# Four block sums of the up-projection weights: one by an adding DMA, two in place, and a new order of the seven products

## The chip, the cores and the metric

The kernel runs on one core of one Trainium2 chip. A core has TensorE (PE in the rows) for matrix products, VectorE (DVE), ScalarE (ACT) and GpSimd (POOL) for elementwise work, and 16 DMA engines that move data between HBM and the on-chip SBUF. SyncE (SP) only issues DMAs here. Each engine works through its own list of instructions in order and waits at semaphores for the others. The metric is the device time of one execution in microseconds (us).

## The reference

The kernel computes an encoder of two layers on a sequence of 512 rows of width 1024. Each layer is a half-step feed-forward block, a token mixer (a convolution module in layer 0, a gated linear recurrence "HGRN2" in layer 1), and a second half-step feed-forward block:

```
def swiglu(h, w13, w2):
    gate, up = jnp.split(h @ w13, 2, axis=-1)
    return (jax.nn.silu(gate) * up) @ w2

for layer in range(DEPTH):                       # DEPTH = 2
    x = x + 0.5 * swiglu(rms_norm(x, ...), ffn_w13[layer, 0], ffn_w2[layer, 0])
    x = x + mix(rms_norm(x, ...))                # conv in layer 0, HGRN2 in layer 1
    x = x + 0.5 * swiglu(rms_norm(x, ...), ffn_w13[layer, 1], ffn_w2[layer, 1])
return rms_norm(x, final_g)
```

There are thus four feed-forward blocks. `w13` has 2 x 2816 columns, in 22 blocks of 128 for the gate and 22 for the up half. The change touches the product `h @ w13` of all four blocks, and the storage of HGRN2's `v`.

## The kernel before

**Products in three parts.** All is fp32. A weight tile is split in `split` (L128-130) into a rounded part `whi` (a ScalarE copy, L129) and the rest `wlo` (a VectorE subtraction, L130); the activations are held as `x7h` and `x7l` in the same way. Each product is three matmuls: high by high, high by low, low by high.

**Seven products for eight.** The up-projections (`h @ w13`) use the Strassen-Winograd scheme: one gate block and one up block, each of 128 columns, form a *pair*, and a pair is one 2 x 2 block product, made with seven block products for eight. There are 86 pairs in all (22 in each of three feed-forward blocks, 20 in the first, where two pairs are done plainly). A pair's raw weights are one 128 x 2048 tile `wraw` of 1 MB with four quarters of 512 columns, a11, a12, a21, a22. SP loads it (L123-124, three buffers). `seven_w` (L154-173) makes four sums on VectorE, each 128 x 512:

- S1 = a21 + a22 and S2 = S1 - a11, in a tile `s12`;
- S4 = a12 - S2 and S3 = a11 - a21, in a tile `s43`.

It splits four weight tiles from these: wa = (S1, S2), wb = (a11, a12), wc = (S4, S3), each 128 x 1024, and wd = a22, 128 x 512 (`wdh`, `wdl`). wa, wb and wc take the `whi`/`wlo` buffers in turn, of which there are three (L152); wd has a buffer of its own.

**Order of the products.** `seven` (L449-456, matmuls at L455) issues one block product: 12 matmuls of 128 x 256. `seven_pair` (L458-509) issues those of a pair, 84 matmuls with wd's, into two PSUM tiles `x` and `y`: wa's first half, wb's first half, then wd of the *previous* pair (in `close`), wa's second half, wb's second half, wc's first and wc's second half. ScalarE copies parts between (L468-469, L492, L497), VectorE adds two 128 x 256 parts (L495, L498, recorded at L149), and the gate is formed in `evac`: t (L523, VectorE), silu (L525, ScalarE), t (L527, VectorE), gh (L528, ScalarE), gl (L529, VectorE). The first pair of a half block has no previous one (`close is None`) and runs its products in another order.

**What sets the order around the change.** The program's order is not the engines' order: the tile framework schedules each engine's list when the program is built, so instructions of pair n+1's weights stand between those of pair n's products. Buffers are taken in turn, and a writer waits until the last reader of the old content is through. In the steady stretches a pair's list repeats with only the buffer numbers changed.

**The other half** of a feed-forward block, `@ w2`, uses plain products with 512 columns (L187-189). Between the blocks come norms, whose sums of squares `ss` are added on POOL (L334).

Of the kernel before, what the change touches and what calls it, by code (L numbers as in the profile page):

```python
# [11 lines left out]
F32 = mybir.dt.float32  # L12
# [3 lines left out]
AF = mybir.ActivationFunctionType  # L16
ALU = mybir.AluOpType

P = 128
D = 1024  # L20
S = 512
# [39 lines left out]
def tile_encoder(ctx: ExitStack, tc: tile.TileContext, xT, vecs, masks, w13, w2, pw1, kout, kout2, win, win_i, out):  # L61
    nc = tc.nc
    cst = ctx.enter_context(tc.tile_pool(name="cst", bufs=1))
    xp = ctx.enter_context(tc.tile_pool(name="xp", bufs=1))
    wp = ctx.enter_context(tc.tile_pool(name="wp", bufs=3))
# [33 lines left out]
    for w_ in win_order:  # L99
        n = int(w_[1:])  # L100
# [4 lines left out]
    plan_kout(1)  # L105
    plan_ffn(3)

    raws = {}
    parts = []
    for ci, (src, sizes) in enumerate(plan):  # L110
        off = 0
# [4 lines left out]
    ready = {}  # L116

    def wdma(upto):
        while state["dma"] < min(upto, len(plan)):
            ci = state["dma"]  # L120
            src, sizes = plan[ci]
            n = sum(sizes)
            t = wp.tile([P, 2048], F32, name="wraw", tag="wraw", bufs=3)  # L123
            nc.sync.dma_start(t[:, :n], src)
            raws[ci] = t
            state["dma"] += 1

    def split(hi, lo, raw, off, a, b):  # L128
        nc.scalar.copy(hi[:, a:b], raw[:, off + a:off + b])  # L129
        nc.vector.tensor_tensor(lo[:, a:b], raw[:, off + a:off + b], hi[:, a:b].bitcast(F32), op=ALU.subtract)  # L130

    def wsplit(upto):
        while state["split"] < min(upto, len(parts)):
            i = state["split"]
            ci, off, sz = parts[i]
            wdma(ci + 1)
            if sz > D:
                ready[i] = seven_w(raws[ci])
                state["split"] += 1
                continue  # L140
            hi = wp.tile([P, D], F32R, name="whi", tag="whi", bufs=3)
            lo = wp.tile([P, D], F32R, name="wlo", tag="wlo", bufs=3)
            raw = raws[ci]
            split(hi, lo, raw, off, 0, sz)
            ready[i] = (hi, lo)
            state["split"] += 1

    def add(o, a, b, op=ALU.add):
        nc.vector.tensor_tensor(o, a, b, op=op)  # L149

    def wtile():
        return [wp.tile([P, D], F32R, name=n, tag=n, bufs=3) for n in ("whi", "wlo")]  # L152

    def seven_w(raw):  # L154


        q = D // 2
        a11, a12, a21, a22 = (raw[:, i * q:(i + 1) * q] for i in range(4))
        s12 = st["R"].tile([P, D], F32, name="s12", tag="s12")
        s43 = st["R"].tile([P, D], F32, name="s43", tag="s43")  # L160
        add(s12[:, :q], a21, a22)
        add(s12[:, q:], s12[:, :q], a11, ALU.subtract)
        wa = wtile()
        split(*wa, s12, 0, 0, D)
        wb = wtile()
        split(*wb, raw, 0, 0, D)
        add(s43[:, :q], a12, s12[:, q:], ALU.subtract)
        add(s43[:, q:], a11, a21, ALU.subtract)
        wc = wtile()
        split(*wc, s43, 0, 0, D)  # L170
        wd = [st["R"].tile([P, q], F32R, name=n, tag=n) for n in ("wdh", "wdl")]
        split(*wd, raw, 3 * q, 0, q)
        return wa, wb, wc, wd
# [21 lines left out]
    st = {}  # L195
# [28 lines left out]
    for k in range(0, KD, 2):  # L224
        sl = slice(k // 2 * P, (k // 2 + 1) * P)
        src = plan[0][0].rearrange("p (g c) -> p g c", g=4)[:, :, sl]
# [55 lines left out]
    norm = {}  # L282
# [166 lines left out]
    def seven(o, w, i, slot, start=False, kps=range(NP)):  # L449

        x = slice(slot * T2, (slot + 1) * T2)
        for kp in kps:
            sl = slice((i * NP + kp) * P, (i * NP + kp + 1) * P)
            for a, b in ((w[0], x7h), (w[0], x7l), (w[1], x7h)):
                nc.tensor.matmul(o, lhsT=a[:, sl], rhs=b[kp][:, x], start=start and kp == 0 and a is w[0] and b is x7h,  # L455
                                 stop=kp == NP - 1 and a is w[1], skip_group_check=True)

    def seven_pair(lead, close, done):  # L458


        wa, wb, wc, wd = wget()
        x, y = psum(), psum()
        l, r = slice(0, T2), slice(T2, S)
        cs = st["R"].tile([P, 3 * T2], F32, name="cs", tag="cs")
        p5, u2, u3 = (cs[:, i * T2:(i + 1) * T2] for i in range(3))

        def seed():
            nc.scalar.copy(y[:, l], x[:, l])  # L468
            nc.scalar.copy(p5, x[:, r])

        if close is None:
            z = psum()
            for kps in (range(NP - 1), range(NP - 1, NP)):
                seven(x[:, r], wa, 0, 1, True, kps)
                seven(x[:, l], wb, 0, 0, False, kps)
                if kps[-1] == NP - 1:
                    seed()
                seven(z[:, l], wb, 1, 2, True, kps)
                seven(z[:, r], wc, 0, 3, False, kps)
            lead.group()  # L480
            zs = tp.tile([P, S], F32, name="t0", tag="t0")
            nc.scalar.copy(zs, z)
            add(x, x, zs)
            seven(y[:, l], wa, 1, 5)
            nc.scalar.copy(u2, y[:, l])
        else:
            seven(x[:, r], wa, 0, 1, True)
            seven(x[:, l], wb, 0, 0)
            seed()
            close()  # L490
            seven(y[:, l], wa, 1, 5)
            nc.scalar.copy(u2, y[:, l])  # L492
            seven(x[:, l], wb, 1, 2)
            seven(x[:, r], wc, 0, 3)
        add(x[:, r], x[:, r], u2)  # L495
        seven(y[:, l], wc, 1, 4)
        nc.scalar.copy(u3, y[:, l])  # L497
        add(y[:, r], u3, p5)  # L498
        if close is None:
            lead.group()  # L500
        wnext()

        def end():
            seven(y[:, l], wd, 0, 6)
            if lead.n == 2:
                lead.group()
            done(x, y)()

        return end
# [314 lines left out]
    def hgrn(next_prep):  # L824
        lead = Lead()
        with tc.tile_pool(name="hn", bufs=1) as hn, ExitStack() as scratch:
            onh = [hn.tile([P, S], F32R, name=f"onh{k}", tag=f"onh{k}") for k in range(NH)]
            onl = [hn.tile([P, S], F32R, name=f"onl{k}", tag=f"onl{k}") for k in range(NH)]
            hp = scratch.enter_context(tc.tile_pool(name="hp", bufs=1))
# [24 lines left out]

            def v_proj(g, hook=None):

                v = hp.tile([P, 4, S], F32, name="v", tag="v")
                acc = [psum() for _ in range(4)]
                for part in range(4):
                    hi, lo = wget()  # L860
                    for c in range(4):
                        for kk in range(2):
                            k = part * 2 + kk
                            ts_ = slice(c * P, (c + 1) * P)
                            sl = slice(kk * S, (kk + 1) * S)
                            nc.tensor.matmul(acc[c], lhsT=xh[k][:, ts_], rhs=hi[:, sl], start=k == 0, stop=False)  # L866
                            nc.tensor.matmul(acc[c], lhsT=xh[k][:, ts_], rhs=lo[:, sl], start=False, stop=False)  # L867
                            nc.tensor.matmul(acc[c], lhsT=xl[k][:, ts_], rhs=hi[:, sl], start=False, stop=k == KD - 1)  # L868
                            if hook is not None:
                                hook()  # L870
                    lead.group()
                    wnext()
                for c in range(4):
                    nc.scalar.activation(v[:, c, :], acc[c], AF.Copy, scale=norm["r4"][:, c:c + 1])
                vt[g] = v

            def q_evac(h, p):
# [48 lines left out]
            def head(h):  # L926
                q, f, k, kd, gg = (T.pop((h, n)) for n in ("q", "f", "k", "kd", "gg"))

                A = hp.tile([P, 4, S // 2], F32, name="A", tag="A")
# [29 lines left out]
                while hl <= 128:  # L959
# [5 lines left out]
                    else:  # L965
                        for i, (s_, d_, t_) in enumerate(((0, 0, 1), (1, 1, 0), (2, 0, 3), (3, 1, 2))):
                            nc.tensor.matmul(sp[:, i * P:(i + 1) * P], lhsT=k[:, d_, s_ * P:(s_ + 1) * P],
                                             rhs=Q[:, 1 - d_, t_ * P:(t_ + 1) * P], start=True, stop=True)
# [47 lines left out]
                kts = hp.tile([P, S], F32, name="kts", tag="kp", bufs=2)  # L1016
                nc.scalar.copy(kts, kt)
                yield WIDE_STEP
                v = vt[h // 4]
                hs = slice((h % 4) * P, (h % 4 + 1) * P)  # L1020
                st = psum("aux")
                for s_ in range(4):
                    d_ = s_ // 2
                    nc.tensor.matmul(st[:, d_ * P:(d_ + 1) * P], lhsT=kts[:, s_ * P:(s_ + 1) * P], rhs=v[:, s_, hs],
                                     start=s_ % 2 == 0, stop=s_ % 2 == 1)
                state = hp.tile([P, 2 * P], F32, name="state", tag="state")
                nc.scalar.copy(state, st[:, :2 * P])
# [3 lines left out]
                for t_ in range(4):  # L1031
                    ot = po[:, t_ * P:(t_ + 1) * P]
                    a_ = t_ // 2
                    for c in (2 * a_, 2 * a_ + 1):
                        nc.tensor.matmul(ot, lhsT=A[:, c, (t_ % 2) * P:(t_ % 2 + 1) * P], rhs=v[:, c, hs],  # L1035
                                         start=c % 2 == 0, stop=False)
                    nc.tensor.matmul(ot, lhsT=Q[:, a_, t_ * P:(t_ + 1) * P], rhs=state[:, (1 - a_) * P:(2 - a_) * P],
                                     start=False, stop=True)
                    if t_ == 1:
                        yield 1  # L1040
# [205 lines left out]
```

## Time and profile before

| what | value |
|---|---|
| median of three runs | 2042.1 us (2040.7 to 2044.1) |
| the profiled execution: its own time, its span | 2041.71 us, 2039.9 us |
| TensorE busy | 1977.2 us, 97% of the span |
| VectorE busy | 1554.6 us, 76% |
| ScalarE busy | 1046.2 us, 51% |
| GpSimd busy | 253.7 us, 12% |
| read from HBM | 178.92 MB |

The span runs from the first to the last recorded instruction; the execution's own time has some 1.8 us more around it. A busy share is an average over stages of different kinds: the 86 pairs, the `w2` products, the two mixers and the norms. The line numbers in rows are those of the kernel before, printed above.

### The profile page before, as it was taken

The numbers are of one execution on the slowest core, as the hardware profiler recorded it, in microseconds if no ns is written. First come the engines' busy times: TensorE is split into PE (matmuls) and PEld (weight loads), VectorE is DVE, ScalarE is ACT, GpSimd is POOL, SyncE is SP. The second block draws the span as 40 slices with busy tenths as digits, with TensorE's granted clock in tenths as the row PEclk, the third lists the DMA queues.
The fourth block names the chain that finished last, engine by engine and source line by source line (L and its number), as shares of the span: only waits on it lengthen the run. The fifth ranks groups of instructions, "written<-read, shape, count | busy, mean of one in ns | idle before, by whom it ended". The sixth has DMA issues, their size and how long they took to land.

```text
span 2039.9 us, 30786 instructions
## 1 busy us (share of the span) xinstructions
PE 1977.2 (97%) x12429; PEld 1754.4 (86%) x12429; DVE 1554.6 (76%) x2337; ACT 1046.2 (51%) x1757; POOL 253.7 (12%) x201
## 2 busy tenths in 40 slices
PE   7999999998889999999999999999999989999997
PEld 6998998765679989988998998888888869989996
DVE  8975985598689848969975985388758879857964
ACT  6652663576456525645642663355545456624642
POOL 2000001399520000001000001011101010000002
PEclk8999999999899999999999999999999999999998
DMA  4223223211112232322333223211111122232321
GB/s 161 100 92 125 84 91 113 97 46 58 41 63 104 99 119 83 104 93 104 106 105 111 99 95 108 103 62 63 62 62 52 53 76 91 91 106 104 105 99 56
DMA packets 33230, 182.99 MB, mean 90 GB/s; under 512 B 3536, under 2 KB 7760, under 8 KB 18112
## 3 DMA queue, kind: packets, MB, share of 16 engines
q1 hardware_dynamic: 32400, 180.04, 25.6%
q8 instruction: 97, 1.59, 0.3%
q10 hardware_dynamic: 544, 0.52, 0.1%
q0 software_dynamic: 144, 0.46, 0.1%
q14 instruction: 45, 0.37, 0.1%
HBM read 178.92 MB, written 2.10 MB: 89 GB/s over the span
## 4 chain that ended last, share of the span: by engine, by line
PE 82%; DVE 9%; POOL 4%; issue 2%; ACT 2%; DMA 0%; SPq 0%; DVEq 0%; POOLq 0%; ACTq 0%
PE mm L455 39%; PE mm L187 11%; PE mm L189 11%; PE mm L188 11%; PE aux L963 3%; POOL ga L689 3%; DVE wlo L130 2%; DVE mm L681 1%; DVE t L305 1%; DVE x7l L149 1%; PE mm L868 1%; PE mm L866 1%; PE mm L867 1%; PE aux L1035 1%; DVE x7l L305 1%
## 5 line engine op out<-in xcount | busy, mean ns | idle before, releaser
L455 PE MATMUL mm<-x7h,whi 128*128 128x256 f32 x2064 | 578.5, 281 | 8.5 <-ACT whi L129 4.8
L455 PE MATMUL mm<-x7h,wlo 128*128 128x256 f32 x2064 | 577.9, 280 | 3.6 <-DVE wlo L130 3.5
L455 PE MATMUL mm<-x7l,whi 128*128 128x256 f32 x2064 | 577.5, 280 | 0.0
L130 DVE TENSOR_TENSOR wlo<-wraw,whi 128x1024 fp32r<-128x1024 f32 (+2 forms) x292 | 319.0, 1092 | 147.5 <-ACT whi L129 142.9
L129 ACT CAST whi<-wraw 128x1024 fp32r<-128x1024 f32 (+2 forms) x292 | 268.7, 921 | 314.0 <-PE mm L188 282.0
L455 PEld LDWEIGHTS mm<-x7h,whi 128*128 128x128 f32 x2064 | 388.0, 188 | 11.5 <-ACT whi L129 6.3
L455 PEld LDWEIGHTS mm<-x7h,wlo 128*128 128x128 f32 x2064 | 387.8, 188 | 5.3 <-DVE wlo L130 5.2
L455 PEld LDWEIGHTS mm<-x7l,whi 128*128 128x128 f32 x2064 | 388.1, 188 | 0.3
L187 PE MATMUL mm<-gh,whi 128*128 128x512 f32 (+1 forms) x715 | 279.4, 391 | 0.0
L189 PE MATMUL mm<-gh,wlo 128*128 128x512 f32 (+1 forms) x715 | 277.9, 389 | 0.0
L188 PE MATMUL mm<-gl,whi 128*128 128x512 f32 (+1 forms) x715 | 275.1, 385 | 0.0
L129 ACT CAST whi<-s 128x1024 fp32r<-128x1024 f32 x172 | 180.5, 1049 | 163.6 <-PE mm L455 119.7
L334 POOL TENSOR_TENSOR ss<-ss,sq 128x512 f32<-128x512 f32 x48 | 70.3, 1464 | 1446.2 <-ACT sq L333 1445.7
L130 DVE TENSOR_TENSOR wlo<-s,whi 128x1024 fp32r<-128x1024 f32 x172 | 210.1, 1221 | 33.6 <-ACT whi L129 32.4
L187 PE MATMUL mm<-xh,whi 128*128 128x512 f32 x384 | 163.1, 425 | 0.0
L189 PEld LDWEIGHTS mm<-gh,wlo 128*128 128x128 f32 x715 | 134.2, 188 | 30.5
L188 PEld LDWEIGHTS mm<-gl,whi 128*128 128x128 f32 x715 | 134.2, 188 | 28.5
L189 PE MATMUL mm<-xh,wlo 128*128 128x512 f32 x384 | 154.7, 404 | 2.5 <-DVE wlo L130 2.5
L187 PEld LDWEIGHTS mm<-gh,whi 128*128 128x128 f32 x715 | 134.5, 188 | 25.4
L188 PE MATMUL mm<-xl,whi 128*128 128x512 f32 x384 | 153.1, 399 | 0.0
L579 DVE TENSOR_TENSOR t<-mm,rs 128x512 f32<-128x512 f32 x63 | 43.5, 690 | 108.4 <-PE mm L189 108.4
L149 DVE TENSOR_TENSOR s<-wraw 128x512 f32<-128x512 f32 x172 | 117.4, 686 | 6.6 <-DMA wraw<-in_w 4.7
(248 smaller groups left out, 3364.6 us busy)
## 6 DMA issues: line engine op xcount, KB each, us to landing
wraw<-in_w SPq DMA_DIRECT2D x87, 1024.0 KB, 4.8
wraw<-in_w SPq DMA_DIRECT2D x64, 704.0 KB, 4.1
wraw<-in_win SPq DMA_DIRECT2D x16, 1024.0 KB, 4.7
wraw<-in_pw SPq DMA_DIRECT2D x8, 1024.0 KB, 4.8
wraw<-in_kout SPq DMA_DIRECT2D x8, 768.0 KB, 4.3
wraw<-in_win_i SPq DMA_DIRECT2D x4, 1024.0 KB, 4.8
x<-in_xT SPq DMA_DIRECT2D x8, 256.0 KB, 5.8
wraw<-in_kout SPq DMA_DIRECT2D x2, 1024.0 KB, 4.8
```

What stands on the lines that cost most here:

```text
L129: nc.scalar.copy(hi[:, a:b], raw[:, off + a:off + b])
L130: nc.vector.tensor_tensor(lo[:, a:b], raw[:, off + a:off + b], hi[:, a:b].bitcast(F32), op=ALU.subtract)
L149: nc.vector.tensor_tensor(o, a, b, op=op)
L187: nc.tensor.matmul(o, lhsT=wh, rhs=ah, start=first, stop=False)
L188: nc.tensor.matmul(o, lhsT=wh, rhs=al, start=False, stop=False)
L189: nc.tensor.matmul(o, lhsT=wl, rhs=ah, start=False, stop=last)
L305: nc.vector.scalar_tensor_tensor(o, a, g, b, op0=ALU.mult, op1=ALU.subtract)
L334: nc.gpsimd.tensor_tensor(norm["ss"], norm["ss"], sq, op=ALU.add)
L455: nc.tensor.matmul(o, lhsT=a[:, sl], rhs=b[kp][:, x], start=start and kp == 0 and a is w[0] and b is x7h, stop=kp == NP - 1 and a is w[1], ...
L579: nc.vector.tensor_tensor(pn, p, norm["rs05"], op=ALU.mult)
L689: nc.gpsimd.tensor_tensor(ga, ga, pr, op=ALU.add)
L963: nc.tensor.matmul(sp[:, c * P:(c + 1) * P], lhsT=kp[:, c * P:(c + 1) * P], rhs=view(Q, hl, c), start=True, stop=True)
```

## The change

S1 is no longer made by VectorE. SP loads a21 a second time into the first half of a new tile `s13` (two buffers), and a DMA that POOL issues loads a22 on top of it with `accum_op=add`. The other three sums stay on VectorE: S3 goes into the second half of `s13`; S2 is written over a11, and S4 over a12, in the raw tile, after wb was split from them. So wa is now (S1, S3), wc is (S2, S4), wb is split before wa, and the tiles `s12` and `s43` are gone. The products take an order that goes with it: wb's first half, wa's first half, wd of the previous pair, wc's first half, wb's second half, wa's second half, wc's second half. HGRN2's `v` (four parts of 512 columns) becomes two tiles of two parts with the buffers of `s13`.

```
             t = wp.tile([P, 2048], F32, name="wraw", tag="wraw", bufs=3)
             nc.sync.dma_start(t[:, :n], src)
             raws[ci] = t
+            if len(sizes) == 1 and n > D:
+                q = D // 2
+                s13 = wp.tile([P, D], F32, name="s13", tag="s13", bufs=2)
+                nc.sync.dma_start(s13[:, :q], src[:, 2 * q:3 * q])
+                nc.gpsimd.dma_start(s13[:, :q], src[:, 3 * q:], accum_op=ALU.add)
+                sums[ci] = s13
...
-    def seven_w(raw):
+    def seven_w(raw, s13):
         q = D // 2
         a11, a12, a21, a22 = (raw[:, i * q:(i + 1) * q] for i in range(4))
-        s12 = st["R"].tile([P, D], F32, name="s12", tag="s12")
-        s43 = st["R"].tile([P, D], F32, name="s43", tag="s43")
-        add(s12[:, :q], a21, a22)
-        add(s12[:, q:], s12[:, :q], a11, ALU.subtract)
-        wa = wtile()
-        split(*wa, s12, 0, 0, D)
         wb = wtile()
         split(*wb, raw, 0, 0, D)
-        add(s43[:, :q], a12, s12[:, q:], ALU.subtract)
-        add(s43[:, q:], a11, a21, ALU.subtract)
+        add(s13[:, q:], a11, a21, ALU.subtract)
+        wa = wtile()
+        split(*wa, s13, 0, 0, D)
+        add(a11, s13[:, :q], a11, ALU.subtract)
+        add(a12, a12, a11, ALU.subtract)
         wc = wtile()
-        split(*wc, s43, 0, 0, D)
+        split(*wc, raw, 0, 0, D)
...
         else:
-            seven(x[:, r], wa, 0, 1, True)
-            seven(x[:, l], wb, 0, 0)
+            seven(x[:, l], wb, 0, 0, True)
+            seven(x[:, r], wa, 0, 1)
             seed()
             close()
-            seven(y[:, l], wa, 1, 5)
+            seven(y[:, l], wc, 0, 5)
             nc.scalar.copy(u2, y[:, l])
             seven(x[:, l], wb, 1, 2)
-            seven(x[:, r], wc, 0, 3)
-        add(x[:, r], x[:, r], u2)
-        seven(y[:, l], wc, 1, 4)
+            seven(y[:, l], wa, 1, 4)
+            seven(x[:, r], wc, 1, 3)
+            add(x[:, r], x[:, r], u2)
         nc.scalar.copy(u3, y[:, l])
         add(y[:, r], u3, p5)
...
-                v = hp.tile([P, 4, S], F32, name="v", tag="v")
+                v = [wp.tile([P, D], F32, name="v", tag="s13", bufs=2).rearrange("p (c s) -> p c s", c=2)
+                     for _ in range(2)]
```

VectorE's list before, over one period in the middle of the first feed-forward block. `wraw_875` is the raw tile of a pair n+1, `wraw_1002` that of n+2, `mm_1004` and `mm_1005` are x and y of pair n; `wlo_1112`, `wlo_1116`, `wlo_1122`, `wdl_1126` belong to wa, wb, wc, wd of pair n+1:

```order
L130 TENSOR_TENSOR wlo_1112<-s12_1107,whi_1111 128x1024
L149 TENSOR_TENSOR s12_1234<-wraw_1002 128x512
L130 TENSOR_TENSOR wlo_1116<-wraw_875,whi_1115 128x1024
L149 TENSOR_TENSOR mm_1004<-mm_1004,cs_1006 128x256
L149 TENSOR_TENSOR s12_1234<-s12_1234,wraw_1002 128x512
L523 TENSOR_TENSOR t0_1174<-mm_1004,rs_466 128x512
L149 TENSOR_TENSOR mm_1005<-cs_1006 128x256
L130 TENSOR_TENSOR wlo_1122<-s43_1108,whi_1121 128x1024
L149 TENSOR_TENSOR s43_1235<-wraw_1002,s12_1234 128x512
L149 TENSOR_TENSOR s43_1235<-wraw_1002 128x512
L527 TENSOR_TENSOR t1_1178<-mm_1005,t2_1176 128x512
L130 TENSOR_TENSOR wdl_1126<-wraw_875,wdh_1125 128x512
```

The same period of VectorE after. `wraw_878` is the raw tile of pair n+1, `wraw_1132` that of n+3; `wlo_1114`, `wlo_1119`, `wlo_1125` belong to wb, wa, wc of pair n+1:

```order
L137 TENSOR_TENSOR wlo_1114<-wraw_878,whi_1113 128x1024
L156 TENSOR_TENSOR wraw_878<-s13_880,wraw_878 128x512
L156 TENSOR_TENSOR mm_1011<-cs_1012 128x256
L156 TENSOR_TENSOR mm_1010<-mm_1010,cs_1012 128x256
L137 TENSOR_TENSOR wlo_1119<-s13_880,whi_1118 128x1024
L156 TENSOR_TENSOR wraw_878<-wraw_878 128x512
L530 TENSOR_TENSOR t0_1180<-mm_1010,rs_472 128x512
L156 TENSOR_TENSOR s13_1134<-wraw_1132 128x512
L137 TENSOR_TENSOR wlo_1125<-wraw_878,whi_1124 128x1024
L534 TENSOR_TENSOR t1_1184<-mm_1011,t2_1182 128x512
L137 TENSOR_TENSOR wdl_1129<-wraw_878,wdh_1128 128x512
L536 TENSOR_TENSOR gl6_1179<-t1_1184,gh6_1178 128x512
```

One sum of four is gone from the period; S2 (into `wraw_878`) stands right behind the `wlo` of wb, with both 128 x 256 adds between it and the `wlo` of wa. The sum S3 (into `s13_1134`) is made from a raw tile three pairs ahead, where the earliest sum before was made from one two ahead.

TensorE's list before, where a pair's products begin after the wb half shown last: `wdh_998`, `wdl_999` are wd of the pair before, `whi_1111`, `wlo_1112` the second half of wa:

```order
L455 MATMUL mm_1131<-x7h3_84,whi_1115 128x256
L455 MATMUL mm_1131<-x7l3_88,whi_1115 128x256
L455 MATMUL mm_1131<-x7h3_84,wlo_1116 128x256
L455 MATMUL mm_1005<-x7h0_81,wdh_998 128x256
L455 MATMUL mm_1005<-x7l0_85,wdh_998 128x256
L455 MATMUL mm_1005<-x7h0_81,wdl_999 128x256
```

TensorE's list after, where wb's first half (`whi_1113`, `wlo_1114`) ends and wa's first half (`whi_1118`, `wlo_1119`) begins, with wd of the pair before (`wdh_1001`, `wdl_1002`) set between:

```order
L460 MATMUL mm_1137<-x7h3_84,wlo_1114 128x256
L460 MATMUL mm_1137<-x7h0_81,whi_1118 128x256
L460 MATMUL mm_1137<-x7l0_85,whi_1118 128x256
L460 MATMUL mm_1011<-x7h0_81,wdh_1001 128x256
L460 MATMUL mm_1011<-x7l0_85,wdh_1001 128x256
L460 MATMUL mm_1011<-x7h0_81,wdl_1002 128x256
L460 MATMUL mm_1137<-x7h0_81,wlo_1119 128x256
```

The first use of wa's `wlo` is now the 18th matmul of a pair, behind 12 of wb, two of wa and three of wd. Last uses move as well: counted from the pair's first matmul, wb is through after 60 matmuls, wa after 72 and wc after 84, where before wa was through after 48 and wb after 60. The interleaving shown repeats in 65 of the 86 pairs; the others are first pairs of a half block, their neighbours and the last ones.

POOL's list, before, had no DMA among the sums of squares of the norms. After, at the second feed-forward block, it reads:

```order
L339 TENSOR_TENSOR ss_5335<-ss_5335,sq_5473 128x512
L131 DMA s13_5522<-in_w13 128x512
L339 TENSOR_TENSOR ss_5335<-ss_5335,sq_5536 128x512
L131 DMA s13_5670<-in_w13 128x512
```

The adding DMA of a pair now stands ahead of the norm's last sum of squares on that queue.

## Rows read from the trace of the kernel before

**Rows 1.** The page: span, and busy time by engine.
```profile
span 2039.9 us, 30786 instructions
PE 1977.2 (97%) x12429; PEld 1754.4 (86%) x12429; DVE 1554.6 (76%) x2337; ACT 1046.2 (51%) x1757; POOL 253.7 (12%) x201
```

**Rows 2.** Chain of waits: start us, length us, work; the longest stretch.
```profile
223.07 86.49 PE mm L455 x732
```

**Rows 3.** Stretches: from:to, length; busy us of each engine; PE clock, DMA share, GB/s.
```profile
223.07:309.56 86.49, 86.48 (x733) 86.47 (x734) 78.90 (x110) 52.59 (x88) 0.00 (x0) 1.00 0.30 100
269.78:279.66 9.88, 9.88 (x86) 9.88 (x85) 9.32 (x15) 6.11 (x10) 0.00 (x0) 1.00 0.32 108
```

**Rows 4.** Groups by line: busy us, mean ns, idle before, what ended it.
```profile
L455 PE MATMUL mm<-x7h,whi 128*128 128x256 f32 x2064 | 578.5, 281 | 8.5 <-ACT whi L129 4.8
L455 PE MATMUL mm<-x7h,wlo 128*128 128x256 f32 x2064 | 577.9, 280 | 3.6 <-DVE wlo L130 3.5
...
L149 DVE TENSOR_TENSOR s<-wraw 128x512 f32<-128x512 f32 x172 | 117.4, 686 | 6.6 <-DMA wraw<-in_w 4.7
```

**Rows 5.** Timeline of VectorE over one pair: start us, length us, work, idle before.
```profile
265.03 0.68 DVE L130 TENSOR_TENSOR wdl<-wraw,wdh 128x512 fp32r<-128x512 f32 x1
...
276.63 1.23 DVE L130 TENSOR_TENSOR wlo<-s,whi 128x1024 fp32r<-128x1024 f32 x1 [0.26 <-ACT whi L129]
277.89 0.69 DVE L149 TENSOR_TENSOR s<-wraw 128x512 f32<-128x512 f32 x1
278.50 1.22 DVE L130 TENSOR_TENSOR wlo<-wraw,whi 128x1024 fp32r<-128x1024 f32 x1
279.64 0.42 DVE L149 TENSOR_TENSOR mm<-mm,cs 128x256 f32<-128x256 f32 x1
279.97 0.68 DVE L149 TENSOR_TENSOR s<-s,wraw 128x512 f32<-128x512 f32 x1
280.57 0.68 DVE L523 TENSOR_TENSOR t<-mm,rs 128x512 f32<-128x512 f32 x1
```

**Rows 6.** Timelines of TensorE and ScalarE in two successive pairs.
```profile
269.78 0.28 PE L455 MATMUL mm<-x7h,whi 128*128 128x256 f32 x1
...
279.67 0.28 PE L455 MATMUL mm<-x7h,whi 128*128 128x256 f32 x1
...
269.87 1.05 ACT L129 CAST whi<-s 128x1024 fp32r<-128x1024 f32 x1 [1.76 <-PE mm L455]
270.82 0.36 ACT L497 COPY cs<-mm 128x256 f32<-128x256 f32 x1
...
275.56 1.04 ACT L129 CAST whi<-s 128x1024 fp32r<-128x1024 f32 x1
```

**Rows 7.** TensorE and VectorE at a stall, at the start of a half block.
```profile
208.80 0.39 PE L455 MATMUL mm<-x7h,wlo 128*128 128x256 f32 x1 [0.59 <-DVE wlo L130]
209.02 0.28 PE L455 MATMUL mm<-x7h,whi 128*128 128x256 f32 x1
...
207.52 1.23 DVE L130 TENSOR_TENSOR wlo<-s,whi 128x1024 fp32r<-128x1024 f32 x1 [2.68 <-ACT whi L129]
```

**Rows 8.** DMA issues: count, KB each, median us from issue to landing.
```profile
wraw<-in_w SPq DMA_DIRECT2D x87, 1024.0 KB, 4.8
...
out_dram<-yt SPq DMA_DIRECT2D x6, 256.0 KB, 2.2
...
t<-in_masks POOLq DMA_DIRECT2D x1, 256.0 KB, 4.2
```

**Rows 9.** The raw tile: its loads, least, median and longest.
```profile
DMA to landing us min/median/max: 3.9/4.7/9.3
```

**Rows 10.** GpSimd and VectorE where the second feed-forward block begins.
```profile
599.08 1.46 POOL L334 TENSOR_TENSOR ss<-ss,sq 128x512 f32<-128x512 f32 x1 [3.07 <-ACT sq L333]
...
605.36 0.16 DVE L340 TENSOR_SCALAR ms<-aux 128x4 f32<-128x4 f32 x1 [0.28 <-PE aux L271]
```

More of the change, by code (lines that the diff above doesn't have):

```diff
@@ L106, in tile_encoder @@
     plan_ffn(3)
-    raws = {}
+    raws, sums = {}, {}
     parts = []
@@ L137, in wsplit @@
             if sz > D:
-                ready[i] = seven_w(raws[ci])
+                ready[i] = seven_w(raws[ci], sums.pop(ci))
                 state["split"] += 1
@@ L473, in seven_pair @@
             for kps in (range(NP - 1), range(NP - 1, NP)):
-                seven(x[:, r], wa, 0, 1, True, kps)
-                seven(x[:, l], wb, 0, 0, False, kps)
+                seven(x[:, l], wb, 0, 0, True, kps)
+                seven(x[:, r], wa, 0, 1, False, kps)
                 if kps[-1] == NP - 1:
@@ L478, in seven_pair @@
                 seven(z[:, l], wb, 1, 2, True, kps)
-                seven(z[:, r], wc, 0, 3, False, kps)
+                seven(z[:, r], wc, 1, 3, False, kps)
             lead.group()
@@ L483, in seven_pair @@
             add(x, x, zs)
-            seven(y[:, l], wa, 1, 5)
+            seven(y[:, l], wc, 0, 5)
             nc.scalar.copy(u2, y[:, l])
-        else:
-            seven(x[:, r], wa, 0, 1, True)
-            seven(x[:, l], wb, 0, 0)
+            add(x[:, r], x[:, r], u2)
+            seven(y[:, l], wa, 1, 4)
+        else:
+            seven(x[:, l], wb, 0, 0, True)
+            seven(x[:, r], wa, 0, 1)
             seed()
             close()
-            seven(y[:, l], wa, 1, 5)
+            seven(y[:, l], wc, 0, 5)
             nc.scalar.copy(u2, y[:, l])
             seven(x[:, l], wb, 1, 2)
-            seven(x[:, r], wc, 0, 3)
-        add(x[:, r], x[:, r], u2)
-        seven(y[:, l], wc, 1, 4)
+            seven(y[:, l], wa, 1, 4)
+            seven(x[:, r], wc, 1, 3)
+            add(x[:, r], x[:, r], u2)
         nc.scalar.copy(u3, y[:, l])
@@ L873, in v_proj @@
                 for c in range(4):
-                    nc.scalar.activation(v[:, c, :], acc[c], AF.Copy, scale=norm["r4"][:, c:c + 1])
+                    nc.scalar.activation(v[c // 2][:, c % 2, :], acc[c], AF.Copy, scale=norm["r4"][:, c:c + 1])
                 vt[g] = v
@@ L1023, in head @@
                     d_ = s_ // 2
-                    nc.tensor.matmul(st[:, d_ * P:(d_ + 1) * P], lhsT=kts[:, s_ * P:(s_ + 1) * P], rhs=v[:, s_, hs],
+                    nc.tensor.matmul(st[:, d_ * P:(d_ + 1) * P], lhsT=kts[:, s_ * P:(s_ + 1) * P], rhs=v[s_ // 2][:, s_ % 2, hs],
                                      start=s_ % 2 == 0, stop=s_ % 2 == 1)
@@ L1034, in head @@
                     for c in (2 * a_, 2 * a_ + 1):
-                        nc.tensor.matmul(ot, lhsT=A[:, c, (t_ % 2) * P:(t_ % 2 + 1) * P], rhs=v[:, c, hs],
+                        nc.tensor.matmul(ot, lhsT=A[:, c, (t_ % 2) * P:(t_ % 2 + 1) * P], rhs=v[c // 2][:, c % 2, hs],
                                          start=c % 2 == 0, stop=False)
```

## The prediction

> **What bounds the kernel now.** I read the page first: TensorE is busy for 97% of the span, VectorE for 76% [rows 1]. Then the chain of waits, to see which stage this holds for. Its longest pieces are stretches of TensorE alone at the up-projections, one in each of the eight half blocks; the row shown is 86.49 us without a break [rows 2]. (The other seven lie between 79 and 87 us.) So in the steady part of a half block nothing but TensorE sets the pace. The table of stretches says how near the others are: over one pair, 9.88 us, TensorE is busy all the time, VectorE for 9.32 and ScalarE for 6.11 [rows 3]. The two matmuls that mark the same place in successive pairs are 9.89 us apart [rows 6], for 84 matmuls: 0.1177 us each. The groups by line then say what could be won: the matmuls of L455 idled 8.5 us before a `whi` product and 3.6 us before a `wlo` product [rows 4], 12.1 us in all 86 pairs, and these lie at the starts of half blocks, as the stall in [rows 7].
>
> **What is removed.** One VectorE add of 128 x 512 per pair, half of the 172 in the group of 686 ns: 86 x 0.686 = 59 us of VectorE work [rows 4]. In the steady stretch TensorE waits for none of it, so it is worth nothing there. At the starts at most 12.1 us can go; there wb needs no sum any more, but the first pair's wa now needs its adding DMA and S3, and wc its two sums behind wb's split, so I count 0, with 3 us either way.
>
> **What is moved: the weight buffers.** wa, wb and wc take three `whi`/`wlo` buffers in turn, so wb of the next pair can be split when this pair's wb is through, and so on. Before, wa was through after 48 matmuls of a pair and was needed at matmul 84, the start of the next: 36 x 0.1177 = 4.24 us for one cast and one subtraction. Now wb is through after 60 and the next wb is needed at 84 for `whi`, 86 for `wlo`: 26 x 0.1177 = 3.06 us, for 0.09 (matmul to cast, 269.78 to 269.87), 1.07 (cast to subtraction, 275.56 to 276.63) and 1.22 to 1.25 [rows 5, 6]: 2.4, enough. wa is the tight one. Its buffer is free after 72, its cast is early enough, but its subtraction stands on VectorE behind wb's subtraction, S2 and both 128 x 256 adds. I follow VectorE from t0, the end of the 60th matmul, start to start:
>
> - matmul to cast 0.09, cast to wb's subtraction 1.07: 1.16 [rows 6, 5];
> - that subtraction to S2, which writes over what it read: 1.26, as from 276.63 to 277.89, where the sum also writes over the subtraction's input [rows 5]. Without such an overlap the row is 1.14 (278.50 to 279.64). I take 1.25;
> - S2 to the first 128 x 256 add 0.60 (279.97 to 280.57);
> - two such adds, 0.33 each (279.64 to 279.97): 0.66. The first reads ScalarE's copy after the product that ends at matmul 72. By 0.09 + 0.95 + 0.36 [rows 6] after t0 + 1.41 it is there at t0 + 2.8, and the add's turn is at t0 + 3.0, so it doesn't wait;
> - wa's subtraction 1.22, its end to TensorE 0.05 (207.52 + 1.23 to 208.80) [rows 5, 7].
>
> The sum is 1.16 + 1.25 + 0.60 + 0.66 + 1.22 + 0.05 = 4.94. TensorE wants this `wlo` at the 18th matmul of the next pair, 24 + 17 = 41 after t0: 41 x 0.1177 = 4.82. It waits 0.12 us. A matmul behind such a wait is followed after 0.22 instead of 0.12 (208.80 to 209.02 in [rows 7]), which is 0.10 more: 0.22 us per pair. The next link, wc's subtraction, comes out at t0 + 7.9 against a need of 66 x 0.1177 = 7.77, and the 0.22 already lost cover that. So VectorE is less busy than before, yet TensorE waits for it once a pair, because its work lies in one row between a buffer's release and its next use. The order repeats in 65 pairs: 65 x 0.22 = 14.3 us. With the gap of 1.14 for 1.26 the wait is 0.01 and the loss at most 0.11 a pair, 7 us; if each of the seven links is 0.02 longer it is 0.35, 23 us.
>
> **What is added: two DMAs a pair.** No adding DMA is in the trace. The nearest rows for 256 KB are 2.2 us (SP, to HBM) and 4.2 us (from POOL), for 1 MB 4.8 [rows 8]. I take 2.2 for a21 and 4.2 for a22 on top, 6.4 in sequence, as low bound 2.2 + 2.2 and as high bound twice 4.8. The buffer of `s13` is free after wa's subtraction, at t0 + 4.9, and S1 is wanted for wa's cast two pairs later, after t0 + 2 x 9.88 + 1.5 = 21.3: 16.4 us, so even 9.6 fit, and I cost them at nothing. The cover is gone above 16 us; then each us more costs one us over two pairs. The 43 MB more that are read (86 x 0.5) fall on DMA engines that are 32% busy in the steady stretch [rows 3].
>
> The Trainium skill, "DMA: Bandwidth & Descriptors", section "Anatomy of one DMA — SWDGE (gpsimd) path", gives 2.0 us plus the bytes at 436 GB/s for a DMA from GpSimd, an estimate of 2.6 us for a22 where the row has 4.2. By either it is hidden.
>
> **What is hastened: the raw loads.** A raw buffer is released by wd's subtraction (265.03 in [rows 5]), and the first sum of the new raw tile reads it. Before, that was S1 at 277.89, 12.2 us after the release at 265.71. Now S3 of that tile stands one turn earlier, ahead of wc's subtraction. Released at about t0 - 1.0 and wanted at t0 + 6.0 (4.94 less 0.05 less 0.08 of overlap, then S4 and the gate's multiply at 0.60 each), it has 7.0 us. A load takes 4.7, at longest 9.3 [rows 9]. Between 256 KB and 1 MB the rows grow by (4.8 - 2.2)/0.75 = 3.5 us per MB, so both added DMAs beside it make 4.8 + 1.7 = 6.5: hidden, with 0.5 us to spare.
>
> **At the block changes.** POOL's adding DMA stands ahead of the last sum of squares of a norm, and it waits for SP's load of a21. That sum ran from 599.08 to 600.54, and what reads it ran at 605.36 [rows 10]: 4.8 us of room for a delay that I put at 2 to 3. Nothing, and 2 us each at three places if it is longer. HGRN2's `v` has the same writers and readers: nothing.
>
> **Sum.** 2041.7 (the profiled execution, 0.4 below the median) + 14.3 = 2056.0. The other terms are 0.
>
> **Rivals.**
> - *The chain is hidden.* The wait of 0.12 is a difference of 4.94 and 4.82, made of seven links read to 0.01 or 0.02 each. If S2 follows in 1.14, and if the restart after so short a wait costs nothing, TensorE never stops: 2042, within 4 us. For it: every link came from VectorE at full load. Against it: an overlap of input and output is there, and the rows with one have 1.25.
> - *The relief counts at the starts.* With wb free of sums, the waits before a `wlo` (3.6 us) go and the rest stays: 2038; all 12.1 gone would be 2030. Against it: wa and wc of a first pair need as many VectorE instructions ahead of them as before, less one.
> - *The raw load becomes the bound.* From a load of 6.86 us upwards the loop of release, load L, S3 (0.60), wc's subtraction (1.14), the gate's multiply (0.60) and wd's subtraction (0.68) is longer than a pair: L + 3.02. With L = 7.5 it is 10.52, 0.64 more a pair: 65 x 0.64 = 42, 2083; with the 9.3 of [rows 9] it would be far beyond. For it: the room shrinks from 12.2 to 7.0 while traffic grows. Against it: 6.5 at full overlap. A late S1 would show the same way, in wa's cast. The Trainium skill, "SBUF — State Buffer", section "SBUF: two separate sides", has a rule that speaks for this: a DMA issued from GpSimd can stand still while VectorE holds the port that both share, since its descriptors are written through it. The same page excludes two-input tensor_tensor from the modes that do so, and all of VectorE's work in [rows 5] is of that kind.
>
> **How the numbers follow.** The forecast, 0.1 to 0.35 us lost per pair, has 0.54: 65 times that is 6.5 to 23, 2048 to 2064. Hidden chain 0.20, relief at the starts 0.12, raw load 0.14. Within 0.2% (4 us), about what a measurement of this kernel can tell from no change, is the hidden chain alone: 0.20. Faster is the relief, 0.12; slower the forecast and the raw load, 0.68. Range 2037 to 2080: it leaves out half of the relief and most of the raw load's case, together under 0.2.
>
> **What would show it.** In the steady stretch the period should be 10.1 for 9.88 us, with an idle time of some 0.1 us before a `wlo` matmul once a pair, at the 18th, ended by wa's subtraction, and the idle time of L455 before `wlo` up from 3.6 to some 10 us or more. VectorE's busy time should fall by 59. No matmul should wait for a cast that waits for the adding DMA, and no S3 for a load. The forecast is wrong if TensorE runs through at 9.88 (the chain is shorter than I added up), or if VectorE's idle time before S3 is ended by a load.

## The result, and the profile after

The changed kernel takes 2088.3 us (median of 5 runs, 2082.5 to 2091.8) against 2042.1 us before: a ratio of 1.0224, 95% interval 1.0213 to 1.0236. It is 46 us slower. The forecast was 2056 us, the range ended at 2080.

The page of the profiled execution (span, then busy time by engine), as in [rows 1]:

```profile
span 2086.5 us, 31292 instructions
PE 2003.4 (96%) x12429; PEld 1763.6 (85%) x12429; DVE 1501.5 (72%) x2251; ACT 1042.2 (50%) x1757; POOL 328.1 (16%) x287
```

VectorE has 86 instructions and 53 us less, TensorE has the same number of matmuls and 26 us more of busy time. That rise is lost time in another dress: a matmul is recorded for 0.28 us while the next one starts after 0.12, so a stop of up to 0.16 us between two of them shows as no idle time at all. The weight loads (PEld) overlap less: each is recorded for 0.19 us and the next starts after 0.12, so at most 0.07 us of a stop stays hidden there. In the groups by line these are the rows that answer to [rows 4] (idle time stands behind the bar):

```profile
L460 PE MATMUL mm<-x7h,wlo 128*128 128x256 f32 x2064 | 585.3, 287 | 15.4 <-DVE wlo L137 15.1
...
L460 PE MATMUL mm<-x7h,whi 128*128 128x256 f32 x2064 | 576.8, 282 | 11.6 <-ACT whi L136 6.2
...
L460 PEld LDWEIGHTS mm<-x7h,wlo 128*128 128x128 f32 x2064 | 387.6, 188 | 35.0 <-DVE wlo L137 30.8
```

The same weight loads of the kernel before:

```profile
L455 PEld LDWEIGHTS mm<-x7h,wlo 128*128 128x128 f32 x2064 | 387.8, 188 | 5.3 <-DVE wlo L130 5.2
```

So TensorE waits for the low parts of the weights at least 30 us longer, by this row. The timeline of VectorE over two pairs in the steady stretch (start, length, work, idle before), to be held against [rows 5], says when:

```profile
251.25 0.68 DVE L137 TENSOR_TENSOR wdl<-wraw,wdh 128x512 fp32r<-128x512 f32 x1
...
254.17 1.23 DVE L137 TENSOR_TENSOR wlo<-wraw,whi 128x1024 fp32r<-128x1024 f32 x1 [1.46 <-ACT whi L136]
255.43 0.69 DVE L156 TENSOR_TENSOR wraw<-s,wraw 128x512 f32<-128x512 f32 x1
256.04 0.42 DVE L156 TENSOR_TENSOR mm<-cs 128x256 f32<-128x256 f32 x1
256.38 0.42 DVE L156 TENSOR_TENSOR mm<-mm,cs 128x256 f32<-128x256 f32 x1
256.71 1.21 DVE L137 TENSOR_TENSOR wlo<-s,whi 128x1024 fp32r<-128x1024 f32 x1
257.85 0.68 DVE L156 TENSOR_TENSOR wraw<-wraw 128x512 f32<-128x512 f32 x1
258.45 0.68 DVE L530 TENSOR_TENSOR t<-mm,rs 128x512 f32<-128x512 f32 x1
259.80 0.69 DVE L156 TENSOR_TENSOR s<-wraw 128x512 f32<-128x512 f32 x1 [0.67 <-DMA wraw<-in_w]
260.41 1.22 DVE L137 TENSOR_TENSOR wlo<-wraw,whi 128x1024 fp32r<-128x1024 f32 x1
...
262.15 0.68 DVE L137 TENSOR_TENSOR wdl<-wraw,wdh 128x512 fp32r<-128x512 f32 x1
```

And TensorE in that pair, where wb's buffer is freed, at wa's and at wc's low part:

```profile
253.01 0.28 PE L460 MATMUL mm<-x7h,whi 128*128 128x256 f32 x1
...
257.71 0.28 PE L460 MATMUL mm<-x7h,wdl 128*128 128x256 f32 x1
257.98 0.38 PE L460 MATMUL mm<-x7h,wlo 128*128 128x256 f32 x1
258.20 0.28 PE L460 MATMUL mm<-x7h,whi 128*128 128x256 f32 x1
...
260.93 0.28 PE L460 MATMUL mm<-x7h,whi 128*128 128x256 f32 x1
261.68 0.39 PE L460 MATMUL mm<-x7h,wlo 128*128 128x256 f32 x1 [0.48 <-DVE wlo L137]
261.90 0.28 PE L460 MATMUL mm<-x7h,whi 128*128 128x256 f32 x1
```

There are two losses. The first is in every pair: wa's subtraction ends at 257.92, and its matmul starts 0.27 us after the one before instead of 0.12, the next one after 0.22: 0.25 us. The second is in some: S3 stood 0.67 us waiting for its raw load, wc's subtraction behind it was late, and TensorE lost another 0.7 us. wd's subtractions of successive pairs, 251.25 and 262.15, are 10.90 us apart here, against the 9.88 of a pair in [rows 3]. From the fourth wd of each half block on there are 54 such periods: 36 take 10.2 to 10.36 us and 18 take longer, up to 11.8. Over the whole execution the waits of S3 for a load come to (total us, times, longest):

```profile
DVE s L156 <- DMA wraw<-in_w: 23.5, 29, 2.3
```

Before, the sums waited 4.7 us for loads [rows 4].

The DMAs (count, KB each, median us to landing) against [rows 8], then the queues (packets, MB, share of 16 engines over the span):

```profile
wraw<-in_w SPq DMA_DIRECT2D x87, 1024.0 KB, 6.2
...
s<-in_w SPq DMA_DIRECT2D x86, 256.0 KB, 2.5
s<-in_w POOLq DMA_DIRECT2D x86, 256.0 KB, 4.1
...
q1 hardware_dynamic: 44784, 202.59, 28.0%
q0 software_dynamic: 12528, 23.01, 6.8%
```

The two added DMAs take what was forecast, 2.5 and 4.1 us. The raw load went from 4.8 to 6.2. The adding DMA holds the engines for 6.8% of the span, 142 us, for 23 MB: 6.2 us per MB. The queue of the plain loads had 25.6% of 2039.9 us for 180.0 MB before: 2.9 us per MB. An added byte costs twice a loaded one. And it comes at the worst place. The issues of POOL and SP in that pair:

```profile
250.82 0.87 POOL L131 DMA_DIRECT2D s<-in_w  x1 [9.27 <-DVE wlo L137]
...
251.96 0.33 SPq L124 DMA_DIRECT2D wraw<-in_w  x1
258.00 0.33 SPq L130 DMA_DIRECT2D s<-in_w  x1
```

The adding DMA is issued 1.1 us before the raw load, and 0.7 to 1.5 us in the pairs that follow: a21's load is issued when wa's subtraction is through, the adding DMA 3 us later, when that load has landed, and the raw load when wd's subtraction is through. (The wait of 9.27 us in the first row is put down to wa's subtraction, but a21's load is what ended last: it landed at 250.26.) All three hang on the same period, so they meet in each.

### The profile page after: what moved, and what is told of

The parts are those of the page before. It is cut to its first block, busy times and chain, and to the rows that moved or that the text cites. A ratio compares the mean times of both kernels' runs of the same rounds, so it can differ in the third digit from the quotient of the medians.

```text
span 2086.5 us, 31292 instructions
## 1 busy us (share of the span) xinstructions
PE 2003.4 (96%) x12429; PEld 1763.6 (85%) x12429; DVE 1501.5 (72%) x2251; ACT 1042.2 (50%) x1757; POOL 328.1 (16%) x287
## 3 DMA queue, kind: packets, MB, share of 16 engines
q0 software_dynamic: 12528, 23.01, 6.8%
## 5 line engine op out<-in xcount | busy, mean ns | idle before, releaser
L136 ACT CAST whi<-wraw 128x1024 fp32r<-128x1024 f32 (+1 forms) x378 | 359.0, 950 | 565.1 <-PE mm L193 298.6
L137 DVE TENSOR_TENSOR wlo<-wraw,whi 128x1024 fp32r<-128x1024 f32 (+1 forms) x378 | 423.7, 1121 | 278.6 <-ACT whi L136 273.9
L460 PE MATMUL mm<-x7h,wlo 128*128 128x256 f32 x2064 | 585.3, 287 | 15.4 <-DVE wlo L137 15.1
L131 POOL DMA_DIRECT2D s<-in_w x86 | 74.5, 869 | 1077.2 <-DVE wlo L137 315.0
L136 ACT CAST whi<-s 128x1024 fp32r<-128x1024 f32 x86 | 90.5, 1052 | 41.6 <-PE mm L460 27.4
L137 DVE TENSOR_TENSOR wlo<-s,whi 128x1024 fp32r<-128x1024 f32 x86 | 104.4, 1214 | 3.9 <-ACT whi L136 3.9
```

The lines of the kernel that those rows point to most:

```text
L131: nc.gpsimd.dma_start(s13[:, :q], src[:, 3 * q:], accum_op=ALU.add)
```

## Experiments

Three theories went into the first runs. A: two losses, the wait for wa's subtraction in each pair and the late raw load. B: the DMAs are the whole loss. C: only VectorE's order costs.

**s1_on_dve: no DMAs.** S1 goes back to VectorE, all else as changed.

```
-                nc.sync.dma_start(s13[:, :q], src[:, 2 * q:3 * q])
-                nc.gpsimd.dma_start(s13[:, :q], src[:, 3 * q:], accum_op=ALU.add)
+        add(s13[:, :q], a21, a22)          # in seven_w
```

> The changed kernel without its two DMAs per pair: S1 is made by VectorE into the same tile s13; products, buffers and in-place sums stay as changed. Theory A (two losses: a wait for wa's subtraction once a pair, 0.33 us x 65 = 21 us, and a late raw load, slowed by the adding DMA, some 20 us): the raw load is back at 4.8 us and no S3 waits for it, the wait for wa stays, period 10.2 us: 2060 to 2070 us. Theory B (the DMAs are the whole loss, the short wait for wa only follows from them): period 9.88 us, 2038 to 2046 us. Theory C (only VectorE's order costs, the late raw loads are hidden behind it): 2085 us or more, as one VectorE add per pair is back.

Measured: 2075.9 us, ratio 1.016 (1.0145 to 1.0176). The steady periods are 10.20 to 10.26 almost throughout (the last of each half block 10.32 to 10.36), for instance (VectorE's timeline, wd's subtractions):

```profile
250.10 0.68 DVE L135 TENSOR_TENSOR wdl<-wraw,wdh 128x512 fp32r<-128x512 f32 x1
...
260.31 0.68 DVE L135 TENSOR_TENSOR wdl<-wraw,wdh 128x512 fp32r<-128x512 f32 x1
```

B falls: without a single added DMA the pair still takes 10.21 us. C falls too: 12 us are gone although VectorE got its work back. The total is 6 us above A's range; 6 us of its loss lie at one place, between the first and the second feed-forward block, and why is open.

**s3_late: S3 behind wc's subtraction.** One ordering edge without a wait, S3 to the `wlo` of wc of two pairs before.

```
-        add(s13[:, q:], a11, a21, ALU.subtract)
+        s3 = add(s13[:, q:], a11, a21, ALU.subtract)
+        if len(wcs) > 1:
+            pin(s3, wcs[-2])
...
```

> The changed kernel with one instruction per pair moved in VectorE's list: S3 of the pair three ahead is queued behind wc's subtraction (it then stands behind wd's), which gives the raw load some 2.3 us more room. Nothing else moves, both DMAs stay. Theory A: S3 waits for no load, the wait for wa stays at 0.33 us a pair, all periods near 10.2 us: 2060 to 2070 us. Theory B (contention of the DMAs, wherever the reader stands): 2080 to 2090 us. Theory C (late loads are hidden): 2085 to 2090 us.

Measured: 2077.1 us, 1.017 (1.0153 to 1.0187). The waits for a load fell, in the view of waits (total us, times, longest), from 23.5 us in 29 waits to

```profile
DVE s L162 <- DMA wraw<-in_w: 8.8, 12, 2.3
```

and in the steady stretch hardly a period is long any more. But the steady one is 10.32 to 10.36, 0.12 above A's. The edge also moved the schedule of TensorE: three matmuls of wb stand ahead of wc's low part where there were four, so wc's subtraction is wanted 0.12 us earlier, and TensorE loses 0.20 us there. A is right on the load and misses this.

**adds_late and both_moves.** The 128x256 adds of a pair are queued behind wa's subtraction of the next one; both_moves has S3 late as well.

```
...
+            wnext()
+            last = [add(y[:, r], u3, p5), add(x[:, r], x[:, r], u2)]
+            if len(was) > made:
+                for ins in last:
+                    pin(ins, was[-1])
...
```

> The changed kernel with the two 128x256 adds of a pair queued behind wa's subtraction of the next one on VectorE, instead of ahead of it; S3 stays ahead of wc's subtraction. Theory A: wa's subtraction starts 0.66 us earlier and TensorE no longer waits for it; wc's subtraction comes out at about t0 + 7.9 against a need of 7.8, so up to 0.2 us a pair stays, and the late raw loads cost their 20 us or more, since nothing covers them: 2060 to 2080 us. Theory B: 2085 to 2090 us. Theory C: 2038 to 2048 us.

> Both moves on VectorE: the two 128x256 adds behind wa's subtraction, S3 behind wc's. Both DMAs stay. Theory A: neither wait is left in the steady stretch, period 9.9 us: 2038 to 2048 us. Theory B: 2080 to 2090 us. Theory C: 2038 to 2048 us, as A.

Measured: adds_late 2069.2 us, 1.0136 (1.0115 to 1.0157); both_moves 2061.9 us, 1.0092 (1.0077 to 1.0107). adds_late is where A put it. both_moves misses A's range by 14 us: in the steady stretch no load is late and no matmul waits for wa, yet the period is 10.15. TensorE in both_moves:

```profile
257.08 0.28 PE L468 MATMUL mm<-x7h,wdl 128*128 128x256 f32 x1
257.20 0.28 PE L468 MATMUL mm<-x7h,whi 128*128 128x256 f32 x1
257.32 0.28 PE L468 MATMUL mm<-x7l,whi 128*128 128x256 f32 x1
257.52 0.38 PE L468 MATMUL mm<-x7h,wlo 128*128 128x256 f32 x1
```

Behind wd stands wc, and its third matmul, the first with the low part, comes 0.20 us after the second. With the adds moved, the schedule of TensorE runs wb, wa, wd, wc in blocks of 12, and wc's low part is wanted as the 39th matmul instead of the 43rd. The wait went from wa to wc.

**plain_dma: a22 loaded, not added.** S1 holds a22 alone; one sum is left out.

```
-                nc.gpsimd.dma_start(s13[:, :q], src[:, 3 * q:], accum_op=ALU.add)
+                nc.gpsimd.dma_start(s13[:, :q], src[:, 3 * q:])
```

> The changed kernel with a plain DMA of a22 from POOL in place of the adding one: S1 holds a22 alone, so one of four sums is left out of the computation, the schedule is the same. In the trace of the changed kernel a 2 KB packet of the adding DMA takes 178 ns of its engine and one of a21's plain load 84. Theory A: with half of that engine time gone, the raw load lands some 0.7 us earlier, S3 waits less, and the wait for wa (0.33 us a pair) stays: 2066 to 2080 us. Theory B: the same direction, 2060 us or less. If the added traffic alone mattered and not the adding: 2085 to 2090 us.

Measured: 2070.8 us, 1.014 (1.0127 to 1.0153), as A had it: 17.5 us of the 46 go with the adding. The same 23.01 MB of POOL's queue hold the DMA engines for 3.1% of the span, 64 us, where the adding ones took 142:

```profile
q0 software_dynamic: 7024, 23.01, 3.1%
```

The packets are fewer too, 4 KB each where the adding DMA's are 2 KB, so the edit changes two things. The size is not the reason: in the changed kernel a21's plain load has packets of 2 KB as well, and one takes 84 ns where an adding one takes 178. In the stretch from 223 to 309 us the raw load lands after (least, median, longest) in the changed kernel

```profile
DMA to landing us min/median/max: 4.9/6.3/7.7
```

and in plain_dma

```profile
DMA to landing us min/median/max: 4.6/5.6/5.9
```

With the same bytes on the same queues at the same places the waits of S3 fall to

```profile
DVE s L156 <- DMA wraw<-in_w: 7.1, 11, 1.6
```

and the steady periods are 10.20 to 10.26, as without any added DMA in s1_on_dve. So I put what is left, 28.7 us, down to the order.

**no_s2_plain.** plain_dma without S2.

```
-        add(a11, s13[:, :q], a11, ALU.subtract)
```

> plain_dma with one VectorE instruction less per pair: S2 is left out (wc is split from a11 and S4 = a12 - a11), and a22 is loaded plainly, so two of the four sums are left out of the computation. On VectorE the way from wb's subtraction to wa's is 0.7 us shorter; TensorE still wants wa's low part at the 18th matmul. Theory A (that chain is what TensorE waits for once a pair): the wait of 0.33 us goes, period 9.9 us, 65 x 0.33 = 21 us less than plain_dma's 2071: 2046 to 2053 us. If another thing made the pair longer: 2065 us or more.

Measured: 2058.7 us, 1.0078 (1.0061 to 1.0094), period 10.15. It doesn't test what it was made for: S4, no longer waiting for S2, took S2's place on VectorE, and the way from wb's subtraction to wa's is as long as it was. VectorE, then TensorE:

```profile
252.02 1.23 DVE L137 TENSOR_TENSOR wlo<-wraw,whi 128x1024 fp32r<-128x1024 f32 x1 [1.57 <-ACT whi L136]
253.28 0.69 DVE L156 TENSOR_TENSOR wraw<-wraw 128x512 f32<-128x512 f32 x1
...
254.56 1.22 DVE L137 TENSOR_TENSOR wlo<-s,whi 128x1024 fp32r<-128x1024 f32 x1
```

```profile
255.55 0.28 PE L459 MATMUL mm<-x7h,wdl 128*128 128x256 f32 x1
255.83 0.38 PE L459 MATMUL mm<-x7h,wlo 128*128 128x256 f32 x1
256.05 0.28 PE L459 MATMUL mm<-x7h,whi 128*128 128x256 f32 x1
```

2.54 us from subtraction to subtraction, as in the changed kernel (254.17 to 256.71), and the same 0.28 and 0.22 at wa's low part. It does separate the links: wa's alone is 10.15 - 9.89 = 0.26 us a pair, and the rest of the 10.21, 0.06, was wc's.

**old_products: the DMA in the old order.** wa = (S1, S2) first, wb second, wc = (S3, S4) from the raw tile.

```
-            seven(x[:, l], wb, 0, 0, True)
-            seven(x[:, r], wa, 0, 1)
+            seven(x[:, r], wa, 0, 1, True)
+            seven(x[:, l], wb, 0, 0)
...
+        add(s13[:, q:], s13[:, :q], a11, ALU.subtract)
```

> S1 by the adding DMA and the other sums in place, as changed, but with the product order of before: wa = (S1, S2) first, wb second, wc = (S3, S4) from the raw tile. So wa's buffer is free after 48 matmuls again and wanted at 84. S2 reads the raw tile after wd's subtraction, so the raw load keeps its wide room. Theory A (order and buffer turn cost 0.33 us a pair, the close reader of the raw load the rest): neither is left, 2036 to 2046 us, although both DMAs run. Theory B (the DMAs cost by contention alone): 2055 to 2065 us, the 10 to 14 us by which the change is slower than its version with S1 on VectorE.

Measured: 2177.6 us, 1.0672 (1.0648 to 1.0696), far outside both. The view of waits names it:

```profile
DVE s L156 <- DMA s<-in_w: 194.2, 65, 6.7
```

Here S2 needs S1 early, and its half of the tile is held until S4 has read it, so a21's load and the adding DMA no longer fit between two uses. The 16 us of lead that the prediction found for them belong to the new product order. So it says nothing on A against B; it says that in this form, with two `s13` buffers, the adding DMA does not fit the old order.

**Other orders of the products.** Two tries to take the waits out of the changed kernel: wb's second half ahead of wc's first (wb_twice_first), and wb, wa, wb, wc, wd, wa, wc with TensorE's list held to that (spread_uses); each also with S1 on VectorE.

```
-            seven(y[:, l], wc, 0, 5)
-            nc.scalar.copy(u2, y[:, l])
             seven(x[:, l], wb, 1, 2)
+            seven(y[:, l], wc, 0, 5)
+            nc.scalar.copy(u2, y[:, l])
```

> The changed kernel with two of the seven products exchanged: wb's second half ahead of wc's first half. wb's buffer is then free after 48 matmuls instead of 60, and wc is wanted at 48 instead of 36. VectorE's list follows: S3 of the pair three ahead falls behind wc's subtraction, the adds behind wa's. Theory A: no wait is left in the steady stretch, period 9.9 us: 2036 to 2046 us. Theory B: 2055 us or more.

> As wb_twice_first, but S1 is made by VectorE and there are no added DMAs. It tells what the adding DMA is worth once the product order leaves room. Theory A: TensorE is the bound either way, VectorE at 9.3 of 9.9 us fits: within 3 us of wb_twice_first. Theory B: 10 us or more faster than wb_twice_first. Theory D (VectorE's relief counts): 3 us or more slower than wb_twice_first.

> The changed kernel with the products of a pair in the order wb first, wa first, wb second, wc first, wd of the pair before, wa second, wc second, and TensorE's list held to it. wb is free after 36 matmuls and wanted at 84, wc free after 84 and wanted at 120, wa free after 72 and wanted at 96 (subtraction at 98: 26 x 0.1177 = 3.06 us for 2.43), and wd's 12 matmuls cover the copy between wc's first and wa's second half. Both DMAs and all sums as changed. Theory A: no wait is left in the steady stretch, period 9.9 us: 2036 to 2048 us. Theory B (the adding DMA costs by itself): 2055 us or more.

> As spread_uses, with S1 made by VectorE and no added DMAs. Theory A: TensorE bounds both, within 4 us of spread_uses. If VectorE's relief by 59 us is worth something in this order: 4 us or more slower than spread_uses. If the adding DMA still costs: faster than spread_uses by 4 us or more.

Measured: wb_twice_first 2062.3 us, 1.0104 (1.0089 to 1.0119), with S1 on VectorE 2066.4, 1.0123 (1.011 to 1.0137); spread_uses 2125.1, 1.0403 (1.0387 to 1.0418), with S1 on VectorE 2125.3, 1.0406 (1.0391 to 1.0422). The times lie in B's ranges, but not for B's reason: no weight and no load is late in the steady stretch of either, and both have a new wait, which I had not counted: a product that writes a PSUM tile must let ScalarE's copy out of it finish. In spread_uses (TensorE, then ScalarE):

```profile
254.99 0.28 PE L460 MATMUL mm<-x7h,wlo 128*128 128x256 f32 x1
256.01 0.39 PE L460 MATMUL mm<-x7h,whi 128*128 128x256 f32 x1 [0.74 <-ACT cs L475]
```

```profile
255.31 0.36 ACT L474 COPY mm<-mm 128x256 f32<-128x256 f32 x1 [1.55 <-PE mm L460]
255.58 0.38 ACT L475 COPY cs<-mm 128x256 f32<-128x256 f32 x1
```

wb's second half follows the copies of x directly, and its first matmul comes 1.02 us after the one before instead of 0.12, in each pair. In wb_twice_first it is the copy u2, and the wait and the restart cost 0.26 us a pair (two steps of 0.27 and 0.23). In the orders before and after wd's or another tile's products cover these copies. The pairs of runs answer the other question: with the same wait in both, the adding DMA is worth 4 us (2062.3 against 2066.4, with intervals that overlap; by the bound set ahead a small relief) or nothing (2125.1 against 2125.3), for 53 us of VectorE. The 4 us do not come from the steady stretch: by wd's subtractions, the 54 steady periods of wb_twice_first are 14.0 us longer than before and those of the version with S1 on VectorE 11.8. None of these versions beats the kernel before.

**traffic_only: both DMAs in the kernel before.** 368 of 512 columns, into a tile that nobody reads.

```
+                q, c = D // 2, 368
+                dm = wp.tile([P, c], F32, name="dm", tag="dm", bufs=1)
+                tc.keep_in_program_order(nc.sync.dma_start(dm, src[:, 2 * q:2 * q + c]))
+                nc.gpsimd.dma_start(dm, src[:, 3 * q:3 * q + c], accum_op=ALU.add)
```

> The kernel before with the two DMAs of the change added as traffic alone: for each pair, right behind the raw load, SP loads 368 of a21's 512 columns into a tile that nobody reads, and POOL adds 368 of a22's columns to it by an adding DMA (72% of the change's bytes, as far as SBUF has room). Product order, sums and the lists of TensorE, VectorE and ScalarE in the steady stretch are those of before, where the first reader of a raw tile has 12.2 us after its release. Theory A (the adding DMA costs only where the raw load's reader stands close): the raw load takes 5.5 to 7 us instead of 4.7, no sum waits for it, period 9.88 us: 2040 to 2046 us. Theory B (the adding DMA costs by contention wherever the reader stands): 2052 us or more, 72% of the 17 us by which the changed kernel is slower than with a plain DMA.

Measured: 2046.5 us, 1.0021 (1.001 to 1.0031), 0.5 us above A's range and far from B's. The sums wait 4.3 us in all for a load, and 4.7 before [rows 4], so with 12 us of room the traffic costs no wait. It is a weaker test than planned, since the adding DMA here mostly runs after the raw load has landed (4.7 us in the median in the stretch from 223 to 309 us, as before [rows 9]). A period is 9.94 us for 9.89, with no wait in it; see the end.

## Why the prediction was wrong

**What bounds the kernel, and the relief.** Right. 53 us of VectorE's work went (59 were counted) and bought nothing in the steady stretch. The starts, counted as 0 with 3 us either way, did not gain but lost; see the last item.

**The weight buffers.** Right in place and mechanism: TensorE stops once a pair at wa's low part, the 18th matmul. The links are as added up: from 253.01, where wb's last product of the pair is through, to wa's subtraction at 256.71 the trace has 3.70 us, where the links of the forecast make 3.67. The wait and restart are 0.25 for 0.22. wc's link, which I had as covered by that loss, cost 0.06 more. Together 0.32 a pair: over 65 pairs 21 us for 14.3. Shown by s1_on_dve, which in the steady stretch has this loss alone, and by no_s2_plain for the two links; its removal only moved the wait (both_moves).

**The two DMAs.** Right: 2.5 and 4.1 us, S1 is waited for nowhere. The Trainium skill, "SBUF — State Buffer", section "SBUF: two separate sides", warns that a DMA from GpSimd starves while VectorE works in a 2-port mode, and excludes tensor_tensor from these modes. The trace agrees: with VectorE at 72% the adding DMA landed after 4.1 us in the median and 3.7 to 6.2 in the steady stretch, and S1 was on time.

**The raw loads.** This step failed: "both added DMAs beside it make 4.8 + 1.7 = 6.5: hidden, with 0.5 us to spare". The room was right (251.93 to 259.05, 7.1 us for 7.0). The load was not: 6.2 in the median, but up to 7.7 in the steady stretch. I priced the added bytes as plain ones, at 3.5 us per MB, where the adding DMA holds the engines twice as long as a plain load, and I took the median of a load against a room that each load has to meet. With a plain DMA in its place the longest load of the stretch was 5.9 us, within the 6.5 that I had (plain_dma). What showed it was the sign named ahead: VectorE's idle time before S3 ended by a load. The rival with the late load had the price right: 7.75 us for the load of 251.96 gives 7.75 + 3.02 = 10.77, and the period was 10.90. Its share is 17.5 us (plain_dma), 12 of them in the 54 periods counted above.

**The block changes.** Right, within 2 us: from the last wd of one feed-forward block to the second of the next the changed kernel takes 0.5 us more, 0.8 less and 2.0 more than before.

**The forms of the cases.** I had set the chain and the late load against each other, with a chance for each. They add: 21 + 17.5 = 38.5 of the 46 us. The other 8, at nothing in my sum, lie where half blocks begin. By wd's subtractions plain_dma, which has the order without the adding, loses 19.0 us against the kernel before in the 54 steady periods, 9.5 between the second and the fourth wd of the eight half blocks, and nothing in the rest. Which waits make these 9.5 stays open.

## What to carry to other kernels

An engine with less work can still make the bound engine wait: what counts is the time from a buffer's release to its next use, and what stands on the queue in that time, not the busy share. A DMA is priced by how long it holds the engines, and an adding one counted double here; then ask which other transfer falls into the same moment of each period, and hold the longest case, not the median, against the room. Cases that use different resources are not rivals; their costs are added.

## What was not expected of the hardware

- A DMA of 256 KB from POOL landed after 4.1 us with the adding and 2.9 without (plain_dma, median of the stretch), and the adding one held the DMA engines for 6.2 us per MB against 2.9 for the raw loads.
- In traffic_only the matmuls of a pair took 9.94 us for 9.89, without a wait of TensorE that the profile shows and at a granted clock of 1.00 in that stretch. From 235 to 295 us the steps from matmul to matmul are 0.1183 us in the mean for 0.1177, and none is over 0.125. Over the 70 periods from the second wd of each half block on that is 3 of the 5 us that this run lost. In that stretch the DMA engines were busy for 43% of the time for 29% before; the cause is open.
